# Block solutions of a gated DeltaNet layer: four systems in four column groups, two chunk pairs in one visit

## The chip, the cores and the metric

The kernel runs on one core of a Trainium2 chip. The metric is the device time of one execution in microseconds (us). The engines are the matrix engine (TensorE, PE in the profile; its weight loads are PEld), VectorE (DVE), ScalarE (ACT), GpSimd (POOL) and SyncE (SP), which issues the DMAs. Each engine works through its instructions in program order and waits on semaphores for the others.

## The reference, cut to what matters

One inference step of two layers, a sliding-window attention layer and a gated DeltaNet (GDN) layer, for 1024 prompt tokens and 8 x 4 sample tokens, model width 1024. The change is in the prompt part of the GDN layer:

```python
def gated_delta_chunked(q, k, v, g, beta, s0, chunk):
    ...
    decay = jnp.exp(jnp.where(incl, gc[..., :, None] - gc[..., None, :], -jnp.inf))
    kb = kc * bc[..., None]
    lower = jnp.where(strict, jnp.einsum('nbhik,nbhjk->nbhij', kb, kc) * decay, 0.0)
    rhs = jnp.concatenate([vc * bc[..., None], kb * jnp.exp(gc)[..., None]], axis=-1)
    sol = lax.linalg.triangular_solve(lower + jnp.eye(chunk, dtype=lower.dtype), rhs,
                                      left_side=True, lower=True, unit_diagonal=True)
    ...
    def step(S, xs):
        w_v_c, w_k_c, qk_c, q_dec_c, k_dec_c, g_tot_c = xs
        u = w_v_c - jnp.einsum('bhck,bhkv->bhcv', w_k_c, S)
        o = jnp.einsum('bhck,bhkv->bhcv', q_dec_c, S) + jnp.einsum('bhij,bhjv->bhiv', qk_c, u)
        S = S * g_tot_c[..., None, None] + jnp.einsum('bhck,bhcv->bhkv', k_dec_c, u)
        return S, o
```

Each value head and chunk has a unit lower triangular system. The kernel uses chunks of 128 tokens (the result does not depend on the chunk): 8 chunks, 16 value heads in 8 head pairs (two value heads share one key head), so 16 systems of 128 x 128 for each head pair. It inverts them once and then runs through the chunks in order, with the state `S`.

## The kernel before

The matrix engine's main work in this layer is the input projection. Column tiles of 128 columns are taken one after another in `plan`; each is 24 matmuls in float32r for each of three token groups (384, 384 and 288 columns; `ps_pj` in the profile, with weights `wh`, `wl` and activations `h2hi`, `h2lo`). For a head pair r the program projects q, two z tiles, the next pair's k, and two v tiles.

Everything else of the layer is written as generators that are woven in between those matmuls (`weave`). The program is laid out at build time: a planner (`Core`) keeps an estimated clock for each engine, and after each projection matmul it lets every generator go on whose next condition holds (`ready`, `soon`, `idle`). Where several could go on, ranks set by hand for each head pair (`KR`) decide. Conditions also hold the projection back (`until`): the k tile of pair r+1 is projected once the chain of pair r-1 is finished, and the pre-activation buffers of the convolution must be free. While it is held back, only woven work is laid out. What comes out is a fixed order for each engine.

For a head pair hq:

- `solve`: transposes of kT (`turn_sum`), key products `kT kT` in PSUM, and their scaled, decayed copy `UZ` (16 systems, four to a chunk pair: two chunks, two heads). The four 32 x 32 diagonal blocks of each system go to DRAM (`Ld`).
- `invert`: all 64 diagonal blocks are inverted at once on VectorE, in 31 steps of two instructions (`tmp`, `X`); the result goes through DRAM (`Xdd`) to `Xc`.
- `blocks`: for a chunk pair, the inverted blocks are masked into `Xd` (GpSimd), multiplied into `M` (PE, four matmuls; copied by ACT), and a 32 x 32 transpose writes them onto the diagonal of `UZ` (VectorE). Three steps of block substitution then fill the rows from 64, 32 and 0 on: each is a visit of four matmuls with 32-column weights `M` and 32, 64 or 96 moving columns of `UZ`, and a copy back. Two `blocks` generators run side by side, each with two chunk pairs one after the other. All four matmuls of a visit write the PSUM partitions of the rows that they fill.
- `decayed`: transposes and products of qT with kT, scaled into `DP`.
- `chain`: chunk by chunk `vo`, u (`ps_ob<-vo,UZ`), `us`, the state update (`us,ktok`), outputs (`S,qT`, `uo,DP`) and `S,kT` for the next chunk; each step alternates between PE and DVE or ACT.

The step in `blocks` that the change rewrites:

```python
                        rs, cs = slice(r0, r0 + 32), slice(r0 + 32, P)
                        for q in range(4):
                            nc.tensor.matmul(pzv[rs, q, cs], M[:, q, rs], uz[:, q, cs], start=True, stop=True)
                        yield soon(pz)
                        nc.vector.tensor_copy(uz[rs, :, cs], pzv[rs, :, cs])
```

After the last column tile the program waits for all `solve`, `invert`, `blocks` and `decayed` work, and then starts the output projection, with the rest of the last chain and the samples woven in. All instructions that pass the planner have line L89 in the profile, so one goes by tile names.

## Time and profile before

| | |
|---|---|
| median of 3 runs | 1768.01 us (1766.73 to 1768.91) |
| the profiled execution | 1762.72 us, span 1760.8 us |
| PE busy | 1670.2 us (95% of the span) |
| PEld busy | 1450.0 us (82%) |
| DVE busy | 1214.9 us (69%) |
| ACT busy | 864.3 us (49%) |
| POOL busy | 603.6 us (34%) |
| mean granted PE clock | 0.986 |

A row of the timeline is start, length, engine, line, operation, output and inputs, form and count; rows of one tile in a row are merged. Matmul ends are modelled, so lengths overlap; the time that a visit takes is read from start to start. A float32 matmul has two records.

### The profile page before, as it was taken

The page shows a single profiled execution, that of the slowest core. Times are in us where ns is not written, and L with a number is a line of the kernel's source. Part 1 is how long each engine was busy: PE and PEld are TensorE (multiplying, and loading weights), DVE is VectorE, ACT ScalarE, POOL GpSimd, SP SyncE. Part 2 cuts the span into 40 slices and gives each one's busy share as a digit, 9 for nine tenths or more (in the row PEclk, how much of TensorE's full clock was granted, in tenths as well). Part 3 has the DMA queues.
Part 4 walks back from the last instruction along what each step waited for, and adds up shares of the span by engine and source line. Part 5 has one row for each costly group of instructions (what it writes and reads, how often), then busy time and mean ns, then how long its engine had stood idle before and what let it go on. Part 6 is the DMA issues. An engine that isn't in the chain of part 4 may idle for free. (4 is left out here: it accounts for less than half of the span.)

```text
span 1760.8 us, 31819 instructions
## 1 busy us (share of the span) xinstructions
PE 1670.2 (95%) x10666; PEld 1450.0 (82%) x10666; DVE 1214.9 (69%) x3538; ACT 864.3 (49%) x2514; POOL 603.6 (34%) x1170
## 2 busy tenths in 40 slices
PE   6999999999998989799999999999999998998897
PEld 5988888877777889679999999899998987766685
DVE  5426676554555678867878778688697884458677
ACT  5525565453334555156554655564656564433332
POOL 2401110112122234344443544444344445323332
PEclk9999999999999999899999999999999999999999
DMA  9442121233333232132422324224133126764885
GB/s 338 131 112 61 49 69 49 67 103 110 102 108 101 62 88 61 52 87 53 115 61 70 95 62 112 60 67 120 39 94 82 45 76 187 240 193 145 265 258 168
DMA packets 281572, 191.77 MB, mean 109 GB/s; under 512 B 98361, under 2 KB 253881, under 8 KB 281378
## 3 DMA queue, kind: packets, MB, share of 16 engines
q1 hardware_dynamic: 281410, 189.75, 37.5%
q8 instruction: 84, 1.38, 0.3%
q14 instruction: 78, 0.64, 0.1%
HBM read 144.68 MB, written 47.04 MB: 109 GB/s over the span
## 5 line engine op out<-in xcount | busy, mean ns | idle before, releaser
L89 PE MATMUL ps_pj<-h2hi,wl 128*128 128x384 f32 (+1 forms) x1128 | 381.1, 338 | 2.7 <-POOL wl L89 2.5
L89 PE MATMUL ps_pj<-h2lo,wh 128*128 128x384 f32 (+1 forms) x1128 | 381.3, 338 | 0.0
L89 PE MATMUL ps_pj<-h2hi,wh 128*128 128x384 f32 (+1 forms) x1128 | 379.4, 336 | 0.6 <-ACT XR L89 0.6
L89 POOL TENSOR_TENSOR wl<-wr,wh 128x512 fp32r<-128x512 f32 x122 | 164.8, 1352 | 545.7 <-ACT wh L89 518.8
L89 PEld LDWEIGHTS ps_pj<-h2hi,wl 128*128 128x128 f32 x1128 | 213.7, 189 | 6.9 <-POOL wl L89 3.6
L89 PEld LDWEIGHTS ps_pj<-h2hi,wh 128*128 128x128 f32 x1128 | 213.5, 189 | 3.9 <-ACT XR L89 0.9
L89 PEld LDWEIGHTS ps_pj<-h2lo,wh 128*128 128x128 f32 x1128 | 213.6, 189 | 3.7
L89 POOL TENSOR_TENSOR xt<-xt,y 128x512 f32<-128x512 f32 (+1 forms) x48 | 63.3, 1323 | 176.0 <-DVE y L89 137.6
L89 PE MATMUL ps_pj<-hlo,wh 128*128 128x384 f32 (+1 forms) x360 | 119.6, 332 | 0.0
L89 PE MATMUL ps_pj<-hhi,wh 128*128 128x384 f32 (+1 forms) x360 | 118.6, 330 | 0.0
L89 PE MATMUL ps_pj<-hhi,wl 128*128 128x384 f32 (+1 forms) x360 | 118.0, 328 | 0.0
L89 DVE SCALAR_TENSOR_TENSOR vT<-XR,cT,vT 128x384 f32<-128x384 f32 (+1 forms) x144 | 90.3, 640 | 37.9 <-ACT vT L89 36.0
L89 DVE TENSOR_TENSOR tmp<-X 64x31 f32<-64x31 f32 (+15 forms) x248 | 91.2, 368 | 15.5 <-POOL X L89 12.3
L89 DVE TENSOR_TENSOR X<-X,tmp 64x31 f32<-64x31 f32 (+15 forms) x248 | 95.2, 384 | 8.5
L89 ACT CAST wh<-wr 128x512 fp32r<-128x512 f32 x122 | 75.1, 616 | 20.9 <-PE ps_pj L89 15.6
L89 PEld LDWEIGHTS ps_pj<-hlo,wh 128*128 128x128 f32 x360 | 67.8, 188 | 13.6 <-issue 13.5
L89 ACT COPY XR<-ps_pj 128x384 f32<-128x384 f32 (+1 forms) x96 | 43.2, 450 | 68.8 <-PE ps_pj L89 68.6
L89 PEld LDWEIGHTS ps_pj<-hhi,wh 128*128 128x128 f32 x360 | 67.7, 188 | 5.9 <-issue 4.2
L89 ACT ACTIVATE qe<-ps_mi,Eg 128x128 f32<-128x128 f32 x112 | 35.1, 364 | 74.4 <-PE ps_mi L89 74.4
L89 PEld LDWEIGHTS ps_pj<-hhi,wl 128*128 128x128 f32 x360 | 67.8, 188 | 3.3 <-issue 3.3
L89 ACT ACTIVATE prob<-prob,nm 128x256 f32<-128x256 f32 (+1 forms) x128 | 62.3, 489 | 11.3 <-DVE nm L89 11.1
L89 POOL TENSOR_TENSOR rst<-rsw 128x4 f32<-128x4 f32 x96 | 22.6, 235 | 128.7 <-DVE rsw L89 106.0
(580 smaller groups left out, 4330.4 us busy)
## 6 DMA issues: line engine op xcount, KB each, us to landing
wr<-in_gdn_w_in SPq DMA_DIRECT2D x96, 256.0 KB
S<-in_state_gdn_s SPq DMA_DIRECT2D x40, 256.0 KB
xt<-in_x_prompt SPq DMA_DIRECT2D x16, 512.0 KB
wm<-in_w_mod SPq DMA_DIRECT2D x16, 512.0 KB
wr<-in_swa_w_in SPq DMA_DIRECT2D x64, 128.0 KB
wm<-in_w_mod SPq DMA_DIRECT2D x32, 256.0 KB
wmod<-in_w_mod SPq DMA_DIRECT2D x32, 256.0 KB
DP<-gcr SPq DMA_DIRECT2D x64, 128.0 KB
```

Of the source, the lines that this page charges most:

```text
L89: inst = fn(*args, **kwargs)
```

## The change

The four `UZ` tiles of a head pair become one tile `full` of [128, 4, 4, 128] (chunk pair, system, columns). One `blocks` generator takes two chunk pairs at a time. A solution step is one visit of eight matmuls for both chunk pairs: system q of each writes PSUM partitions 32q to 32q+31, that is column group q of the array, and the two chunk pairs lie side by side in the columns. The copy back is four instructions, one for each q, from partitions 32q to the rows r0, for both chunk pairs: even q on VectorE, odd q on ScalarE. `decayed` waits for all products instead of for the fourth tile, and uses a scratch tile of its own in `turn_sum`. The ranks and the planner's costs stay.

```diff
-                jk = gs.tile([P, P], F32, tag="jk", name="jk")
+                jk = gs.tile([P, P], F32, tag="jk" if ktok is None else "jn", name="jk")
...
+            full = st["UZf"] = half(hq).tile([P, 4, 4, P], F32, tag="UZ", name="UZ", bufs=1)
+            nc.wide[full.tensor.name] = 8 * P
...
-                    ut = half(hq).tile([P, 2, 2, P], F32, tag="UZ", name="UZ", bufs=4)
+                    uv = full[:, cp_]
+                    ut = uv.rearrange("p (h c) i -> p h c i", h=2)
...
+            st["built"] = True
             weave(invert(hq, st, Ld, Xdd), "invert", hq)
...
-            def blocks(par):
-                for cp_ in (par, par + 2):
-                    xd = Xd[par]
+            def blocks():
+                for c2 in range(2):
                     yield soon(Xc)
-                    for b in range(4):
...
+                    for xd, cp_ in zip(Xd, (2 * c2, 2 * c2 + 1)):
+                        for b in range(4):
...
+                    Ms = []
+                    for xd, cp_ in zip(Xd, (2 * c2, 2 * c2 + 1)):
+                        yield ready(xd)
+                        pm = yield from bank(lg)
...
                     for r0 in (64, 32, 0):
-                        yield ready(M, uz)
+                        yield ready(*Ms, full[:, 2 * c2])
                         pz = yield from bank(lg)
-                        pzv = pz.rearrange("p (q i) -> p q i", q=4)
-                        rs, cs = slice(r0, r0 + 32), slice(r0 + 32, P)
+                        rs, cs, n = slice(r0, r0 + 32), slice(r0 + 32, P), 96 - r0
+                        pzv = pz[:, 0:2 * n].rearrange("p (s i) -> p s i", s=2)
+                        for s_, M in enumerate(Ms):
+                            for q in range(4):
+                                nc.tensor.matmul(pzv[32 * q:32 * q + 32, s_, :], M[:, q, rs], full[:, 2 * c2 + s_, q, cs],
+                                                 start=True, stop=True, skip_group_check=True)
+                        yield soon(pz)
                         for q in range(4):
-                            nc.tensor.matmul(pzv[rs, q, cs], M[:, q, rs], uz[:, q, cs], start=True, stop=True)
-                        yield soon(pz)
-                        nc.vector.tensor_copy(uz[rs, :, cs], pzv[rs, :, cs])
+                            d = full[rs, 2 * c2:2 * c2 + 2, q, cs]
+                            if q % 2:
+                                nc.scalar.copy(d, pzv[32 * q:32 * q + 32])
+                            else:
+                                nc.vector.tensor_copy(d, pzv[32 * q:32 * q + 32])
                         give(lg, pz)
-                st["ready"] = st.get("ready", 0) + 1
-                solved[0] += 1
...
+                st["ready"] = st.get("ready", 0) + 2
+                solved[0] += 2
...
-            yield lambda: st.get("qTdone") and "sj" in st and len(st["UZ"]) == 4
+            yield lambda: st.get("qTdone") and "built" in st
```

The planner lays all of the layer out anew. Three places of PE's order, and one of DVE's, follow; a count behind a row is of instructions.

Pair 4, first chunk pairs, PE, before (`Xd,UZ` is the product for `M`, `UZ,M` a solution step):

```order
L89 MATMUL ps_lg<-Xd_6510,UZ 128x96 x4
L89 MATMUL ps_pj<-h2hi,wh 128x384
L89 MATMUL ps_lg<-UZ,M 32x32 x4
L89 MATMUL ps_pj<-h2lo,wh 128x384
L89 MATMUL ps_pj<-h2hi,wl 128x384
L89 MATMUL ps_pj<-h2hi,wh 128x384
L89 MATMUL ps_pj<-h2lo,wh 128x384
L89 MATMUL ps_pj<-h2hi,wl 128x384
L89 MATMUL ps_lg<-UZ,M 32x32 x4
L89 MATMUL ps_pj<-h2hi,wh 128x384
L89 MATMUL ps_lg<-UZ,M 32x64 x4
```

Now:

```order
L89 MATMUL ps_lg<-UZ,M 32x32 x8
L89 MATMUL ps_pj<-h2hi,wl 128x384
L89 MATMUL ps_pj<-h2hi,wh 128x384
L89 MATMUL ps_pj<-h2lo,wh 128x384
L89 MATMUL ps_pj<-h2hi,wl 128x384
L89 MATMUL ps_pj<-h2hi,wh 128x384
L89 MATMUL ps_pj<-h2lo,wh 128x384
L89 MATMUL ps_pj<-h2hi,wl 128x384
L89 MATMUL ps_pj<-h2hi,wh 128x384
L89 MATMUL ps_pj<-h2lo,wh 128x384
L89 MATMUL ps_pj<-h2hi,wl 128x384
L89 MATMUL ps_lg<-UZ,M 32x64 x8
```

One visit of eight stands where two of four stood, with projections between the steps as before; pairs 2, 3, 5 and 6 have mostly the same picture.

Pair 0, PE, at the k projection of pair 2, which is held back until the chain of pair 0 is finished; before:

```order
L89 MATMUL ps_pj<-h2lo,wh 128x288
L89 MATMUL ps_pj<-h2hi,wl 128x288
L89 MATMUL ps_mi<-Xd_6510,UZ 128x96 x4
L89 MATMUL ps_mi<-UZ,M 32x32 x8
L89 MATMUL ps_mi<-UZ,M 32x64 x8
L89 MATMUL ps_mi<-UZ,M 32x96 x8
L89 MATMUL ps_ob<-vo,UZ 128x128 x2
L89 MATMUL ps_mi<-us,ktok 128x256
```

Now:

```order
L89 MATMUL ps_pj<-h2hi,wl 128x288
L89 MATMUL ps_lg<-qT,kT 128x128 x4
L89 MATMUL ps_mi<-Xd_6508,UZ 128x96 x4
L89 MATMUL ps_mi<-Xd_6510,UZ 128x96 x4
L89 MATMUL ps_mi<-UZ,M 32x32 x8
L89 MATMUL ps_mi<-UZ,M 32x64 x8
L89 MATMUL ps_mi<-UZ,M 32x96 x8
L89 MATMUL ps_mi<-Xd_6508,UZ 128x96 x4
L89 MATMUL ps_mi<-Xd_6510,UZ 128x96 x4
L89 MATMUL ps_mi<-UZ,M 32x32 x8
L89 MATMUL ps_mi<-UZ,M 32x64 x8
L89 MATMUL ps_mi<-UZ,M 32x96 x8
```

Before, 50 projection matmuls stand between the first product of pair 0 and this place; now all its blocks stand behind the last of them. At the end of the column tiles (pair 7) it is the same: all its blocks now stand behind the last projection.

Pair 5, chunk 3 of the chain, PE, before:

```order
L89 MATMUL ps_mi<-us,ktok 128x256
L89 MATMUL ps_pj<-h2lo,wh 128x384
L89 MATMUL ps_pj<-h2hi,wl 128x384
L89 MATMUL ps_tr<-cst,vo 128x128 x4
L89 MATMUL ps_mi<-S,qT 128x256
L89 MATMUL ps_mi<-uo,DP 128x128 x2
L89 MATMUL ps_pj<-h2hi,wh 128x384
L89 MATMUL ps_mi<-S,kT 128x256
L89 MATMUL ps_pj<-h2lo,wh 128x384
```

Now, from chunk 4 on, ahead of the k projection of pair 7:

```order
L89 MATMUL ps_pj<-h2hi,wl 128x288
L89 MATMUL ps_ob<-vo,UZ 128x128 x2
L89 MATMUL ps_mi<-us,ktok 128x256
L89 MATMUL ps_mi<-S,qT 128x256
L89 MATMUL ps_mi<-uo,DP 128x128 x2
L89 MATMUL ps_mi<-S,kT 128x256
L89 MATMUL ps_ob<-vo,UZ 128x128 x2
L89 MATMUL ps_tr<-cst,vo 128x128 x4
L89 MATMUL ps_mi<-us,ktok 128x256
```

and DVE in the same chunks:

```order
L89 TENSOR_SCALAR us<-ps_ob,sd 128x128 x2
L89 TENSOR_TENSOR tmp<-X 64x231
L89 TENSOR_TENSOR X<-X,tmp 64x11x21
L89 SCALAR_TENSOR_TENSOR mo<-mo,epq 128x4
L89 TENSOR_SCALAR rsw<-mo 128x4
L89 TENSOR_SCALAR rsw<-rsw 128x4
L89 SCALAR_TENSOR_TENSOR S<-S,Gt,ps_mi 128x128 x2
L89 TENSOR_TENSOR tmp<-X 64x220
L89 TENSOR_TENSOR X<-X,tmp 64x10x22
L89 TENSOR_TENSOR tmp<-X 64x207
L89 TENSOR_TENSOR X<-X,tmp 64x9x23
L89 SCALAR_TENSOR_TENSOR vo<-ps_mi,nEg,vo 128x128 x2
```

The last four chunks now stand with no projection between, and the inversion steps of pair 6 stand between their steps on DVE. Pair 2's last three chunks (ahead of the k projection of pair 4) stand alike, with transposes of qT, products of `decayed` and the products for `M` of pair 3 among them; and at one v projection each of pairs 3 and 4 three or four pieces of woven work stand in one row with no projection between.

36 lines of the change are left out of this document (16 added, 20 removed).

## The prediction

> **What bounds the kernel now.** I read the page first, then the busy time by stage, then the waits of the matrix engine (PE), then single visits in the timeline.
>
> ```profile
> span 1760.8 us, 31819 instructions
> PE 1670.2 (95%) x10666; PEld 1450.0 (82%) x10666; DVE 1214.9 (69%) x3538; ACT 864.3 (49%) x2514; POOL 603.6 (34%) x1170
> ```
>
> ```profile
> 707.00:781.00 74.00, 61.31 (x445) 48.56 (x444) 57.36 (x165) 23.13 (x79) 26.76 (x87) 0.93 0.26 69
> 781.00:1478.20 697.20, 683.63 (x4682) 640.11 (x4681) 550.39 (x1509) 399.05 (x1243) 321.49 (x779) 1.00 0.30 79
> ```
>
> The columns are the stretch, its length, the busy time of PE, its weight loads, DVE, ACT and POOL, the granted clock, and DMA. The edited code runs in these two stretches. From 781 to 1478 us, where head pairs 2 to 7 are solved, PE is busy 98% and VectorE (DVE) 79%. The waits of PE in that stretch:
>
> ```profile
> PE ps_tr L89 <- ACT vT L89: 3.5, 4, 1.7
> ...
> PE ps_pj L89 <- POOL wl L89: 0.2, 1, 0.2
> ```
>
> These are the first and last of seven (total, times, longest), 13 us together of 697. PE is the bound there: a PE microsecond saved is one of span, as long as projection matmuls (`ps_pj`) stand between the steps that wait for other engines. From 707 to 781 us it is otherwise:
>
> ```profile
> 722.04 1.03 PE L89 MATMUL ps_mi<-Xd,UZ 128*128 128x96 f32 x8
> ...
> 728.86 0.71 PE L89 MATMUL ps_ob<-vo,UZ 128*128 128x128 f32 x4
> ...
> 773.79 0.42 PE L89 MATMUL ps_pj<-h2hi,wh 128*128 128x384 f32 x1
> ```
>
> From 722.04 to 773.79 PE projects nothing; the chain of pair 0 runs from 728.86, and DVE, busy 57 of 74 us, sets the pace.
>
> The sum is made against the profiled execution (1762.7 us, span 1760.8), 5.3 us under the median 1768.0; I add the 5.3 at the end.
>
> **The solution visits.** A visit is four matmuls of one solution step, among projections:
>
> ```profile
> 709.01 0.34 PE L89 MATMUL ps_pj<-h2lo,wh 128*128 128x384 f32 x1
> 709.28 0.44 PE L89 MATMUL ps_mi<-UZ,M 128*32 128x32 f32 x8
> 709.64 0.44 PE L89 MATMUL ps_pj<-h2hi,wl 128*128 128x384 f32 x1
> ...
> 711.09 0.63 PE L89 MATMUL ps_mi<-UZ,M 128*32 128x64 f32 x8
> 711.65 0.44 PE L89 MATMUL ps_pj<-h2lo,wh 128*128 128x384 f32 x1
> 711.93 0.34 PE L89 MATMUL ps_pj<-h2hi,wl 128*128 128x384 f32 x1
> 712.10 0.34 PE L89 MATMUL ps_pj<-h2hi,wh 128*128 128x384 f32 x1
> ...
> 713.62 0.85 PE L89 MATMUL ps_mi<-UZ,M 128*32 128x96 f32 x8
> 714.40 0.44 PE L89 MATMUL ps_pj<-h2hi,wl 128*128 128x384 f32 x1
> ```
>
> From start to start a visit takes 0.36, 0.56 and 0.78 us for 32, 64 and 96 columns (two records for each matmul). A projection matmul takes 0.174 (711.93 to 712.10), but 0.27 ahead of a visit and 0.28 behind one, so each visit costs another 0.2. A head pair has four of each width: 4 x 1.70 = 6.8 us, and twelve crossings.
>
> Afterwards six visits hold eight matmuls each, going round the four column groups. Before has no such visit of these sizes; the nearest that go round four groups are these:
>
> ```profile
> 31.85 3.64 PE L350 MATMUL ps_mi<-wm,cT 128*32 128x512 f32 x32
> 394.24 0.33 PE L89 MATMUL ps_lg<-kxs,qz 64*32 64x32 f32 x16
> 394.39 0.62 PE L89 MATMUL ps_lg<-KT,qz 64*32 64x128 f32 x16
> 394.94 0.44 PE L89 MATMUL ps_pj<-hhi,wh 128*128 128x384 f32 x1
> ...
> 1497.37 0.64 PE L89 MATMUL ps_lg<-S,zq 128*32 128x256 f32 x8
> 1497.94 0.50 PE L89 MATMUL ps_pj<-h2hi,olo 128*128 128x512 f32 x1
> ```
>
> In one column group a record's time grows by 0.053 us per 64 columns ((0.78 - 0.36)/8 from 32 to 96), so 512 columns would take 0.43; the first row has 32 such records in 3.64, 0.11 each. Four groups do overlap. Sixteen records of 32 columns took 0.15 and of 128 columns 0.55, on half the rows of the array; eight of 256 columns, on all rows, 0.57. Scaled by columns both give about 0.15, 0.28 and 0.42 for the new visits. Bounds of a pair's six visits: 1.7 us by those rows, and 6.8 if a record costs 0.57/8 = 0.071 whatever its width (16 records are 1.14, six visits 6.8: no gain at all). I take 1.9, near the lower end, because the 32-column row shows records at 0.01. So 4.9 us are saved, and 1.0 for six crossings fewer (0.2 each, less because some visits of before stand together): 5.9 per pair.
>
> [...]
>
> **Evacuation.** Twelve DVE copies per pair become twelve smaller ones and twelve on ScalarE (ACT).
>
> ```profile
> L89 DVE COPY UZ<-ps_lg x84: 287/417/547, 763.4 to 1479.0; 32x128 f32<-32x128 f32 x28, 32x256 f32<-32x256 f32 x28, 32x384 f32<-32x384 f32 x28
> L89 POOL TENSOR_TENSOR Xd<-Xc,cst x128: 442/452/831, 703.7 to 1469.3; 32x128 f32<-32x128 f32 x128
> L89 DVE TENSOR_TENSOR tmp<-X x248: 172/356/1493, 637.6 to 1445.3; 64x31 f32<-64x31 f32 x8, 64x87 f32<-64x87 f32 x8, 64x135 f32<-64x135 f32 x8, 64x175 f32<-64x175 f32 x8
> L89 DVE TENSOR_TENSOR X<-X,tmp x248: 182/367/1523, 637.9 to 1445.5; 64x31 f32<-64x31 f32 x8, 64x87 f32<-64x87 f32 x8, 64x135 f32<-64x135 f32 x8, 64x175 f32<-64x175 f32 x8
> L89 ACT COPY XR<-ps_pj 128x384 f32<-128x384 f32 x64 | 30.5, 477 | 51.1 <-PE ps_pj L89 51.0
> ```
>
> DVE: before 4 x (0.29 + 0.42 + 0.55) = 5.0; after 4 x (0.22 + 0.29 + 0.35) = 3.4 at 64, 128 and 192 elements on the same slope: 1.6 less. ACT: twelve at 0.2 to 0.48 (the row is larger than any of them), about 3.5 us more per pair. Both lie beside PE work, since ACT is busy 399 of 697 us; without that cover a step waits for two copies in series, some 0.6 us. Eight GpSimd products now stand in one row instead of four: the weight splits behind them come up to 4 x 0.45 = 1.8 us later; they feed projections, and splits are made a column tile ahead. No DMA is added, and the joined tile takes the memory of the four. `decayed` starts at most four products (1.4 us) later; the chain also waits for the solutions, which end later. These cost nothing.
>
> **What moves.** The planner lays everything out anew with the old ranks. Five pairs (2 to 6) are solved among projections as before: 5 x 5.9 = 29.5 us gained. What is given back stands at places where the new order has no projection.
>
> Pair 5, last four chunks (ahead of the K projection of pair 7): chained steps alone, with the next pair's inversion in DVE's row. Chain steps alone before, by the start of `us`, and one chunk among projections:
>
> ```profile
> 736.46 0.59 DVE L89 TENSOR_SCALAR us<-ps_ob,sd 128x128 f32<-128x128 f32 x2
> 742.90 0.59 DVE L89 TENSOR_SCALAR us<-ps_ob,sd 128x128 f32<-128x128 f32 x2
> 752.59 0.61 DVE L89 TENSOR_SCALAR us<-ps_ob,sd 128x128 f32<-128x128 f32 x2 [0.25 <-PE ps_ob L89]
> 756.86 0.61 DVE L89 TENSOR_SCALAR us<-ps_ob,sd 128x128 f32<-128x128 f32 x2 [0.25 <-PE ps_ob L89]
> ```
>
> ```profile
> 971.33 0.61 PE L89 MATMUL ps_ob<-vo,UZ 128*128 128x128 f32 x4
> 971.70 0.42 PE L89 MATMUL ps_pj<-h2lo,wh 128*128 128x384 f32 x1
> ...
> 976.82 0.34 PE L89 MATMUL ps_pj<-h2hi,wl 128*128 128x384 f32 x1
> 976.99 0.60 PE L89 MATMUL ps_ob<-vo,UZ 128*128 128x128 f32 x4
> ```
>
> Alone a chunk takes 6.4 us with many inversion steps between, 4.8 on average over the next two (the inversion ends in the first), and 4.3 without. Among projections it is 5.66 us with 20 projections of 0.174 in it: 2.2. Three periods of 5.6 and an end of 2 are 19 us; the same work among projections would be 4 x 2.2 + 1.5 = 10. Given back: 9 (5 to 12). Pair 2, last three chunks, with more filled in (about 3.4 us of other PE work): 2 x 4.8 + 2.5 = 12 against 10: 2 (0 to 4). At two V projections (pairs 3 and 4) three transposes of `vT` and the next products stand with no projection between; by the longest such wait, 1.7 us, that is 2 and 4 (together 1 to 10).
>
> Pair 0: before, its blocks begin 50 projections ahead of the place without projections; now all of them stand in it. DVE there: 4 transposes (0.71 each, 2.8), some 18 inversion steps of 0.72 (13) and copies (3.4) in one row, 19 us; then the chain, 45 us as before (728.86 to 773.79), with pair 1's blocks inside; 65 projections of 0.174 and one more product, 12. That is 76 against the 74 us of the stretch quoted, although its visits are shorter; 3 with a slower clock (-5 to 8). Pair 7: all its blocks stand behind the last projection, two halves of 5.7 us (products 1.6, ACT and DVE round 1.3, three steps of 0.2 to 0.4 with 0.6 of copies) against 12 us now among projections: 0 (-4 to 4).
>
> The clock falls in such places. The longest wait of PE on `us` in the whole span, and two pieces of the place of pair 0:
>
> ```profile
> PE ps_mi L89 <- DVE us L89: 9.6, 11, 1.5
> ```
>
> ```profile
> 730.00:740.00 10.00, 5.93 (x21) 4.66 (x22) 9.52 (x29) 0.75 (x2) 0.00 (x0) 0.72 0.00 1
> 750.00:760.00 10.00, 7.44 (x37) 4.99 (x36) 5.88 (x21) 4.54 (x18) 4.41 (x17) 1.00 0.50 116
> ```
>
> The granted clock was 0.72 with PE busy 59% and 1.00 with 74%. At periods of 5 to 6 us I expect both; DVE hides most of it. [...]
>
> Everywhere else PE arrives 4% earlier while DVE has nearly the same work: (550 - 10)/668 = 81% instead of 79%. I add 4 us to the 13 of scattered waits (0 to 10).
>
> Sum: -29.5 + 9 + 2 + 6 + 3 + 0 + 4 = -5.5 us. 1762.7 - 5.5 + 5.3 = 1762.5; I predict 1763.
>
> **Rivals.**
> 1. The places without projections are cheap: if chunks there run at 4.3 us, pair 0's blocks finish with the inversion ahead of them, and scattered waits don't grow, 5 + 0 + 2 - 3 + 0 = 4 are given back: 25 gained, 1743. For it: 4.3 was seen. Against: the order puts inversion steps between.
> 2. DVE becomes the bound (slower): the last chunks at 6.4 (12), pair 2 4, V places 10, pair 0 8, scattered 10: 44 against 29.5, 1780 at most, 1775 likely. It decides from 5.9 us per pair given back on average. For it: DVE was 95% busy at 730 to 740 with PE at 59%, and the inversion is not made shorter. Against: 79% over the long stretch.
> 3. The gain is the crossings only (a record costs 0.071 whatever its width): 5 given by five pairs, 24 given back, 1787. Against: 0.01 per record at 394 us.
> 4. Loads of the four groups in line: a record cannot be faster than its load; in the quoted 3.64 us row 0.11 per record leaves that open, but in the 0.57 us one eight records took 0.071 each. At 0.071 it is rival 3's time, 1787. The 394 us rows load half the rows of the array and do not exclude it for 128; the 3.64 us row overlaps whole matmuls on 128. [...]
>
> **How the numbers follow.** A change of 0.2% (3.5 us) is about what a measurement of this kernel can tell. The forecast (net -13 to +3) has 0.45: 0.30 of it faster, 0.15 same. Rival 1 has 0.17, faster. Rival 2 has 0.28: 0.22 slower, 0.06 same. Rivals 3 and 4 together 0.10: 0.09 slower, 0.01 same. Faster 0.47, same 0.22, slower 0.31. The forecast's own range is 1755 to 1771. The range for 8 in 10 goes halfway and more into rivals 1 and 2: 1746 to 1781.
>
> **What would show it.** Right: the rows `UZ,M` drop to under 0.5 us from the start of a visit to the next projection at all three widths; the stretch with pairs 2 to 7 is shorter by 10 us or more although PE's waits in it go from 13 to about 30 us, most of them on DVE `us`, `S`, `vo` and ACT `vT`; the place without projections at pair 0 grows from 52 to about 62 us. Wrong: visits at 1.1 us (rivals 3, 4); PE waits as few as now (rival 1); PE waits over 45 us and DVE over 85% in the long stretch (rival 2). It would also be wrong if the last stage, from 1478 us, moves by more than a few us: I left it as it is.

## The result, and the profile after

The changed kernel takes 1809.96 us (median of 4 runs, 1807.78 to 1813.55) against 1767.37 for the kernel before on the same chip: a ratio of 1.0236 (95% interval 1.0217 to 1.0254), 42 us slower. 1763 was forecast, and the range ended at 1781.

The head of the page of the changed kernel, with busy time, share and instructions of each engine:

```profile
span 1809.0 us, 31894 instructions
PE 1667.1 (92%) x10666; PEld 1444.5 (80%) x10666; DVE 1200.5 (66%) x3538; ACT 888.9 (49%) x2610; POOL 594.0 (33%) x1170
```

The span grew by 48.2 us. PE's busy time fell by 3.1 and its idle time grew from 90.6 to 141.9, by 51.3. So the loss is waiting, not work. (The mean granted clock fell from 0.986 to 0.962, and matmuls at the lower clock count longer: sixteen records of the products `Xd,UZ` take 4.09 us at half clock in a row further down, against 1.03 for eight in the kernel before. That is one reason why so little of what the visits save shows in busy time.)

The stretches by stage: the place of pair 0 without projections, and from its end to the end of pair 7's blocks (length, busy PE, PEld, DVE, ACT, POOL, clock, DMA). Before:

```profile
721.90:773.80 51.90, 39.21 (x260) 29.95 (x258) 41.34 (x126) 17.66 (x63) 14.40 (x52) 0.90 0.22 58
773.80:1478.90 705.10, 691.53 (x4754) 646.30 (x4753) 556.24 (x1523) 402.24 (x1254) 323.55 (x784) 1.00 0.30 79
```

After:

```profile
705.40:788.90 83.50, 53.00 (x382) 40.49 (x381) 61.47 (x193) 24.06 (x85) 24.98 (x85) 0.69 0.19 43
788.90:1523.40 734.50, 684.53 (x4711) 638.28 (x4709) 545.89 (x1519) 424.40 (x1334) 326.01 (x798) 0.96 0.30 81
```

The place grew by 31.6 us and the long stretch by 29.4; the place begins 16.5 us earlier, because pair 0's blocks, which stood in part ahead of it, now stand in it. In the long stretch DVE went from 79% to 74%, so it didn't become the bound. What PE waits for from 705 to 1528 us after (total, times, longest):

```profile
PE ps_mi L89 <- POOL Xd L89: 13.6, 1, 13.6
PE ps_lg L89 <- POOL Xd L89: 13.0, 4, 7.4
PE ps_mi L89 <- DVE us L89: 10.7, 11, 1.6
PE ps_mi L89 <- DVE UZ L89: 7.4, 5, 2.4
PE ps_lg L89 <- ACT UZ L89: 5.4, 2, 2.8
```

All its rows together are 80.8 us; before, the same view from 707 to 1478.2 us sums to 25.3. The two rows at the top are new: PE waits for the masked inverse `Xd`, which comes late.

Among projections the visits did what was forecast (PE, pair 4's first chunk pairs, eight matmuls to a visit, two records each):

```profile
1132.86 0.33 PE L89 MATMUL ps_lg<-UZ,M 128*32 128x32 f32 x16
1133.12 0.44 PE L89 MATMUL ps_pj<-h2hi,wl 128*128 128x384 f32 x1
...
1135.06 0.43 PE L89 MATMUL ps_lg<-UZ,M 128*32 128x64 f32 x16
1135.42 0.45 PE L89 MATMUL ps_pj<-h2hi,wh 128*128 128x384 f32 x1
...
1138.23 0.54 PE L89 MATMUL ps_lg<-UZ,M 128*32 128x96 f32 x16
1138.69 0.57 PE L89 MATMUL ps_lg<-Xd,UZ 128*128 128x96 f32 x3
```

From start to start 0.26, 0.36 and 0.46 us for eight matmuls, against 0.36, 0.56 and 0.78 for four before: 2.2 us per pair instead of 6.8. Where the step before has only just ended, with no projections between, it is otherwise. A visit of pair 1's blocks, inside pair 0's place and at full clock:

```profile
784.15 1.50 PE L89 MATMUL ps_lg<-UZ,M 128*32 128x96 f32 x16
785.59 0.71 PE L89 MATMUL ps_ob<-vo,UZ 128*128 128x128 f32 x4
```

It takes 1.43 us. Its matmuls wait for the copies of the step before one by one: the first four start at 784.15, 784.53, 784.85 and 785.14, the last three of them just behind copies that end at 784.48, 784.79 and 785.09.

So most of the time went into places where PE has no projection. Their lengths, from the start of the last projection matmul ahead to that of the first behind (the forecast's 6 for the V projections was what they would be longer; they were 1.0 together before):

| place | forecast | before | after |
|---|---|---|---|
| pair 0 | 62 | 51.9 | 83.6 |
| pair 2, last chunks | 12 | under 3 | 16.0 |
| V projections, pairs 3 and 4 | 6 | under 1 each | 4.6 + 6.6 + 9.8 |
| pair 5, last chunks | 19 | under 3 | 23.2 |
| pair 7 | 12 | 12.8 (in two) | 33.6 |
| sum | 111 | | 177.4 |

### The profile page after: what moved, and what is told of

It is laid out like the page before. It is cut to its first block, busy times and chain, and to the rows that moved or that the text cites. A ratio compares the mean times of both kernels' runs of the same rounds, so it can differ in the third digit from the quotient of the medians.

```text
span 1809.0 us, 31894 instructions
## 1 busy us (share of the span) xinstructions
PE 1667.1 (92%) x10666; PEld 1444.5 (80%) x10666; DVE 1200.5 (66%) x3538; ACT 888.9 (49%) x2610; POOL 594.0 (33%) x1170
## 5 line engine op out<-in xcount | busy, mean ns | idle before, releaser
L89 PE MATMUL ps_pj<-h2lo,wh 128*128 128x384 f32 (+1 forms) x1128 | 377.0, 334 | 0.0
L89 DVE SCALAR_TENSOR_TENSOR vT<-XR,cT,vT 128x384 f32<-128x384 f32 (+1 forms) x144 | 96.4, 682 | 55.7 <-ACT vT L89 53.9
L89 PEld LDWEIGHTS ps_pj<-hlo,wh 128*128 128x128 f32 x360 | 67.7, 188 | 13.6 <-issue 13.5
L89 POOL TENSOR_TENSOR Xd<-Xc,cst 32x128 f32<-32x128 f32 x128 | 60.7, 474 | 29.5 <-DMA Xc<-Xdd 22.0
```

The source lines that it names most:

```text
L89: inst = fn(*args, **kwargs)
```

## Experiments

Ratios are to the kernel before, run on the same chip. Where an edit changes what the planner sees, it lays out another order, and that turned out to be most of the matter.

### Is it the instructions or the order?

**e1: the changed kernel with one number of the planner's bookkeeping changed.** `nc.wide` tells the planner how many columns of a joined tile it is to treat as one thing: 8 x 128 are two chunk pairs, 4 x 128 one. No instruction is added or removed but for the bookkeeping ones of another order.

```diff
-            nc.wide[full.tensor.name] = 8 * P
+            nc.wide[full.tensor.name] = 4 * P
```

> The changed kernel with one number changed: the planner's key of the joined tile covers one chunk pair (4 x 128 columns) instead of two (8 x 128). No instruction changes, only the planner's order. Theory A (the key): with the wide key the planner lets the products that fill a chunk pair wait for the transfers that read the pair beside it, so the inversion of pair 0 starts 140 projections later and the blocks of pairs 0 and 7 and the last chunks of pair 5 fall behind the last projection. By A the blocks go back to projections 605, 2908 and 3305, the waits of PE on Xd (26.6 us) vanish, and the cheap visits are left: before minus 25 to 33 us, 1735 to 1745. Theory B (the copies, or DVE, are the bound wherever the blocks stand): the visits hardly pay, 1765 to 1800. Theory C (the array: a record of the four groups costs as much as one group's): 1770 to 1790.

Measured: 1760.59 us, ratio 0.997 (0.9957 to 0.9983). One number of the layout gives back 49 us (47 by the ratios), and what is left of the change is 0.3% faster than before. That is far from theory A's 1735 to 1745.

```profile
span 1751.7 us, 31900 instructions
PE 1645.1 (94%) x10666; PEld 1430.1 (82%) x10666; DVE 1202.3 (69%) x3538; ACT 888.6 (51%) x2610; POOL 602.9 (34%) x1170
```

PE is busy 25.1 us less than before (the forecast said 29.5 for the visits), with the very instructions that in the order of the change came to 3.1 less. But its span is only 9.1 shorter: PE's idle time grew by 16.0, from 90.6 to 106.6. So even in this order most of what the visits save is waited for elsewhere.

**e5: the changed kernel without the column groups** (joined tile, wide key and the new wait of `decayed` kept; visits, copies and `blocks` as before). **e2: the kernel before with the joined tile alone** (there `decayed` keeps its old condition and may replace the decay factors before the last products have used them; so part of the result is computed with other factors).

```diff
 e5, against the changed kernel
-            def blocks():
-                for c2 in range(2):
+            def blocks(par):
+                for cp_ in (par, par + 2):
...
+                            nc.tensor.matmul(pzv[rs, q, cs], M[:, q, rs], uz[:, q, cs], start=True, stop=True)
+                        nc.vector.tensor_copy(uz[rs, :, cs], pzv[rs, :, cs])
 e2, against the kernel before
+            full = st["UZf"] = half(hq).tile([P, 4, 4, P], F32, tag="UZ", name="UZ", bufs=1)
+            nc.wide[full.tensor.name] = 8 * P
-                    ut = half(hq).tile([P, 2, 2, P], F32, tag="UZ", name="UZ", bufs=4)
+                    ut = full[:, cp_].rearrange("p (h c) i -> p h c i", h=2)
```

> The changed kernel without the column groups: the joined tile with its wide key and the later start of the decayed products, but two generators, one chunk pair in a visit, one column group and one DVE copy a visit, as before. It repeats the joined tile alone (1804.65 us), with the wait for the last product of the tile put back. If the key alone makes the loss, 1795 to 1808, and the difference to the changed kernel (1810) is what the visits brought less what they moved. If that first run was slow because the decayed products ran too early, it falls to 1770 to 1785.

> The kernel before with nothing but the joined tile and its wide key: visits in one column group, two generators, as before. Theory A (the key): pair 0's blocks lose their projections (604 to 648 of before become 648), the second half of pair 1's and 2's blocks move too, pair 7's stay at 3318 to 3361; so about the 8 us that the changed kernel had lost by the end of pair 1's chain, and 4 to 10 more for its longer visits without cover: 1776 to 1788. Theories B and C: the tile is innocent, 1765 to 1771.

Measured: e5 1805.49, 1.0213 (1.0184 to 1.0242), place of pair 0 86.7 us; e2 1804.65, 1.0218 (1.0198 to 1.0239), place 85.1. The joined tile with its wide key costs 38 us with no solution visit touched. e5 came as the key theory had it; e2 lies 17 us above what was expected of it.

**Where the key bites.** The sixteen scaled key products of pair 0 (`UZ<-ps_mi,sj,DP`) on DVE and the first inversion step (`tmp<-X`, 64x31) behind them; a row that has x8 is eight in one go. Before:

```profile
618.79 2.15 DVE L89 SCALAR_TENSOR_TENSOR UZ<-ps_mi,sj,DP 128x128 f32<-128x128 f32 x8
621.19 2.16 DVE L89 SCALAR_TENSOR_TENSOR UZ<-ps_mi,sj,DP 128x128 f32<-128x128 f32 x8 [0.24 <-PE ps_mi L89]
637.65 0.18 DVE L89 TENSOR_TENSOR tmp<-X 64x31 f32<-64x31 f32 x1 [3.60 <-POOL X L89]
```

The changed kernel:

```profile
616.29 2.15 DVE L89 SCALAR_TENSOR_TENSOR UZ<-ps_mi,sj,DP 128x128 f32<-128x128 f32 x8
622.85 1.39 DVE L89 SCALAR_TENSOR_TENSOR UZ<-ps_mi,sj,DP 128x128 f32<-128x128 f32 x5 [4.42 <-PE ps_mi L89]
628.24 0.34 DVE L89 SCALAR_TENSOR_TENSOR UZ<-ps_mi,sj,DP 128x128 f32<-128x128 f32 x1
645.12 0.35 DVE L89 SCALAR_TENSOR_TENSOR UZ<-ps_mi,sj,DP 128x128 f32<-128x128 f32 x1
646.70 0.34 DVE L89 SCALAR_TENSOR_TENSOR UZ<-ps_mi,sj,DP 128x128 f32<-128x128 f32 x1
657.30 0.18 DVE L89 TENSOR_TENSOR tmp<-X 64x31 f32<-64x31 f32 x1
```

e1:

```profile
616.67 4.45 DVE L89 SCALAR_TENSOR_TENSOR UZ<-ps_mi,sj,DP 128x128 f32<-128x128 f32 x16
633.32 0.18 DVE L89 TENSOR_TENSOR tmp<-X 64x31 f32<-64x31 f32 x1 [2.02 <-POOL X L89]
```

In `solve` a DMA reads the diagonal blocks of each finished chunk pair out of `UZ`. By the planner's code, with one key for two chunk pairs the plan takes the next product, which writes the other chunk pair, for a write into what the DMA still reads, and puts other work ahead of it. The last product ends 28 us after the first eight were done, and the inversion began 20 us later than before although projections ran earlier. Then the rest follows in PE's order:

```profile
705.75 0.72 PE L89 MATMUL ps_lg<-qT,kT 128*128 128x128 f32 x5
720.02 1.38 PE L89 MATMUL ps_mi<-Xd,UZ 128*128 128x96 f32 x5 [13.55 <-POOL Xd L89]
...
743.52 1.22 PE L89 MATMUL ps_ob<-vo,UZ 128*128 128x128 f32 x4
...
788.91 0.42 PE L89 MATMUL ps_pj<-h2hi,wh 128*128 128x384 f32 x1
```

and on GpSimd, where the product itself waits for the inverse on its way through DRAM:

```profile
718.25 0.44 POOL L89 TENSOR_TENSOR Xd<-Xc,cst 32x128 f32<-32x128 f32 x1 [12.18 <-DMA Xc<-Xdd]
```

Projections end at 705.3; 14.7 us pass until the first block product, the blocks take 23.5 (720.02 to 743.52), the chain 45.4.

**e18: narrow key for pair 0 alone.** From pair 2 on its order is that of the changed kernel.

```diff
-            nc.wide[full.tensor.name] = 8 * P
+            nc.wide[full.tensor.name] = (4 if hq == 0 else 8) * P
```

> The changed kernel with the narrow key (4 x 128) for head pair 0's joined tile alone; all other pairs keep the wide one (8 x 128). Its order differs from the changed kernel's only up to the 762nd projection matmul of the layer; from pair 2 on the steps stand at the same projections. Theory (the late products of pair 0 are what makes its place long): the sixteen products stand in one row on VectorE again, the inversion of pair 0 starts some 20 us earlier, the 13.6 us wait of PE on Xd falls below 5, the place goes from 83.6 to 62 to 74 us, and the time from 1810 to 1788 to 1800; the places of pairs 2 to 7 (16.0, 11.2, 9.9, 23.2, 33.6) stay within 3 us each, and they carry the other 27 to 37 us of the 49 that the narrow key gave on all pairs. Rival 1: all blocks of pair 0 still stand behind the last projection, so the place stays over 79 us and the time over 1804; pairs 2 to 7 carry nearly all. Rival 2: pair 0 carries nearly all, under 1775.

Measured: 1805.56 us, 1.0232 (1.021 to 1.0253): not told apart from the changed kernel. The inversion starts at 638.45 (18.9 us earlier), PE's wait ahead of the blocks is 1.8 us instead of 13.55, and the place falls to 69.2 us, as the theory had it:

```profile
638.45 0.18 DVE L89 TENSOR_TENSOR tmp<-X 64x31 f32<-64x31 f32 x1 [3.79 <-POOL X L89]
714.12 0.29 PE L89 MATMUL ps_pj<-h2hi,wl 128*128 128x288 f32 x1
716.22 1.83 PE L89 MATMUL ps_mi<-Xd,UZ 128*128 128x96 f32 x8 [1.80 <-POOL Xd L89]
783.35 0.42 PE L89 MATMUL ps_pj<-h2hi,wh 128*128 128x384 f32 x1
```

But the time did not follow: the place now begins at 714.1 instead of 705.3, so that 8.8 of the 14.4 us were only moved ahead of it, and 5.6 were won (place ends 783.3 and 788.9). The other places stayed (16.1, 4.7 + 6.5, 9.8, 23.6, 33.1). By the time of each projection against the kernel before, the changed kernel stands at +11.6 us behind pair 0's place and at +39.0 at the last projection compared; e1 goes from -6.5 to -15.7 over the same ones. Of their distance of 55, 18 arise up to the end of pair 0's place, of which this run won 6, and 37 behind it: 15 from there to the last projection, in pairs 1 to 6, and 22 at pair 7's place. The place went as the theory had it, the time as rival 1 had it.

The products are late in the other pairs too. Time from the start of a pair's first product to the end of its sixteenth, in us:

| pair | 0 | 1 | 2 | 3 | 4 | 5 | 6 | 7 |
|---|---|---|---|---|---|---|---|---|
| before | 4.6 | 9.0 | 7.5 | 5.5 | 4.2 | 7.1 | 9.9 | 7.4 |
| changed kernel | 30.8 | 15.0 | 20.3 | 11.3 | 8.0 | 20.2 | 18.8 | 9.4 |
| e1 | 4.5 | 9.2 | 8.5 | 4.9 | 4.7 | 9.2 | 14.3 | 7.3 |

That does not yet make them the cause of the time lost there. At pair 7 the key is not enough: e5 has the same key, and there the inversion of pair 7 begins behind 3109 projections (3130 before, 3219 in the changed kernel) and its place is 8.2 us long. In e5, 17 of the 38 us arise up to the end of pair 0's place and about 20 behind it, nearly all of them ahead of the last projection.

**e8 and e9: pair 0's inversion put first on DVE** (rank 21 to 0), in e1 and in the kernel before.

```diff
-    KR = [{'chain': 8, 'output': 9, 'solve': 5, 'invert': 21, 'blocks': 10, 'decayed': 0}, ...
+    KR = [{'chain': 8, 'output': 9, 'solve': 5, 'invert': 0, 'blocks': 10, 'decayed': 0}, ...
```

> The kernel with the narrow key and one rank changed: the inversion of pair 0 goes first (rank 0 instead of 21). The order then has the blocks of pair 0 at projections 384 to 463 and its chain at 506 to 648; no stretch of 58 us without projections is left, and pair 1's blocks stand at 864 to 937. In that stretch of the narrow key PE was busy 45 of 58 us, 9 us of that lost to the half clock: 13 + 9 = 22 us are to be had at most if PE is what bounds the rest. Theory A (what counts is whether projections stand between the steps): 12 to 22 us faster than the narrow key's 1760, 1738 to 1748. Theory B (DVE and the chain's length bound the kernel; what is saved at one place is waited for at the next): 0 to 6 us, 1754 to 1762.

> The kernel before with the same one rank (inversion of pair 0 first): blocks of pair 0 at projections 384 to 420, its chain at 468 to 630. In the 52 us without projections PE was busy 53 of 66 us (708 to 774), about 4 us of it lost to the half clock: 13 + 4 = 17 us at most. Theory A: 9 to 17 us faster than before, 1750 to 1758. Theory B: 0 to 5 us, 1762 to 1767. The difference to the narrow key with this rank is what the visits bring where no place is left without projections: 29 us by the prediction's sum, 5 to 10 if their gain is taken back by waits at the value projections.

Measured: e8 1777.89, 1.008 (1.0061 to 1.01); e9 1773.63, 1.0056 (1.0034 to 1.0078). Both are slower than the kernels they were made from, which no theory had. In e8 the blocks were put so early that PE ran into them among the projections:

```profile
PE ps_mi L89 <- POOL Xd L89: 19.3, 1, 19.3
```

So this earlier order was no gain: the plan had a step ready before the chip did.

### Does the clock make the place of pair 0 long?

Windows (length, busy PE, PEld, DVE, ACT, POOL, clock, DMA) of the changed kernel:

```profile
708.00:710.00 2.00, 0.00 (x0) 0.00 (x0) 1.81 (x6) 0.00 (x0) 0.00 (x0) 1.00 0.54 163
710.00:712.00 2.00, 0.00 (x0) 0.00 (x0) 1.79 (x7) 0.00 (x0) 0.00 (x0) 0.74 0.00 0
712.00:714.00 2.00, 0.00 (x0) 0.00 (x0) 1.83 (x9) 0.00 (x0) 0.00 (x0) 0.50 0.00 0
...
711.00:762.00 51.00, 28.89 (x168) 22.22 (x168) 37.80 (x121) 8.50 (x30) 12.05 (x42) 0.50 0.13 27
```

The clock halved in the idle of 13.55 us and stayed so for 51 us. **e6 and e7** put matmuls that nobody reads into pair 0's place to hold the clock up, in the changed kernel and in e1.

```diff
+    def warm(src, n, w=256):
+        t = psb("pj")
+        for _ in range(n):
+            nc.tensor.matmul(t[:, 0:w], src[:, 0:P], src[:, 0:w], start=True, stop=True)
 e6: ahead of the first products 13 of 512 columns, then two of 256 behind each visit and each u of pair 0
 e7: two of 256 behind the visits of the second half and behind each u of pair 0
```

> The changed kernel with work added to PE at pair 0's place alone: matmuls whose result nobody reads, 13 of 512 columns ahead of the first product of the blocks (into the wait of 13.6 us), 2 of 256 columns behind each solution visit and behind each product of UZ in the chain; the order of all other instructions is unchanged. In the changed kernel the clock was at half from 711 to 762 us, with PE busy 29 us of it. Theory D (the clock makes part of the loss): the clock stays full there, the blocks and the first three chunks run at the speed of the later ones, 14 us of busy time at most are saved, of which 4 or 5 are eaten where PE now arrives late: 8 to 11 us faster than the changed kernel, 1799 to 1802. Theory E (PE waits for DVE, ACT, GpSimd and transfers there, so that its speed doesn't matter): no gain, and the added matmuls delay it by 2 to 8 us, 1811 to 1818.

> The kernel with the narrow key and the same added matmuls at pair 0's place (2 of 256 columns behind each solution visit of its second half and behind each product of UZ in its chain; none ahead of the blocks, which have no long wait there). The narrow key had 24 us at half clock there, PE busy 18.6 us. Theory D: 4 to 8 us faster than the narrow key's 1760.6, 1752 to 1757. Theory E: 1760 to 1766.

Measured: e6 1807.49, 1.022 (1.0192 to 1.0249); e7 1759.98, 0.9965 (0.9946 to 0.9984). In e6 half-clock time at pair 0 falls from 51.2 to 13.6 us (mean granted clock of the execution 0.962 and 0.975) and the place goes from 83.6 to 83.0; in e7 from 24 to 6.8 (0.976 in e1, 0.979 in e7), and the place stays at 58.2. The lower clock in the place is real, but holding it up shortened nothing, as theory E had it: the place goes by its waits for `Xd`, DVE and GpSimd. (The filling matmuls stand in PE's row and may themselves cost part of what the clock gives; that was not separated.)

### What do the four copies cost?

**e4 and e17: all copies on DVE** instead of DVE and ACT in turn, in e1 (order laid out anew) and in the changed kernel (its order kept, by charging the planner the old costs).

```diff
-                            if q % 2:
-                                nc.scalar.copy(d, pzv[32 * q:32 * q + 32])
-                            else:
-                                nc.vector.tensor_copy(d, pzv[32 * q:32 * q + 32])
+                            nc.vector.tensor_copy(d, pzv[32 * q:32 * q + 32])
```

> As the kernel with the narrow key, but all four copies of a visit on DVE. In the profile of the changed kernel the copies of one visit go DVE, ACT, DVE, ACT, each waiting 0.25 to 0.4 us for the one before. Theory A: among projections this series is hidden, so DVE alone makes no difference beyond the new order: within 6 us of the narrow key with both engines. Theory B (copies and DVE bound): twelve more DVE copies of 0.28 us a pair are 3.4 us a pair, 20 to 27 us slower than with both engines.

> The changed kernel in its own order, with all four copies of a visit on DVE (the planner is still charged for two on ACT). In the changed kernel DVE waited 27 us (48 times) for ACT's copies and ACT 68 us (87 times) for DVE's. Theory H: 5 to 15 us faster than the changed kernel, 1795 to 1805; the order, with its stretches without projections, keeps the rest of the loss. If the turns of the copies cost nothing here: 1806 to 1814.

Measured: e4 1757.1, 0.9953 (0.9939 to 0.9968), the fastest of the kernels here that compute all of it, 0.5% faster than before; e17 1805.14, 1.0215 (1.0193 to 1.0237). Each lies a little under its parent, with intervals that overlap, so a gain from it is not shown.

**e3 and e12: column groups for one chunk pair at a time** (four matmuls and four copies in place of four matmuls and one), with the order laid out anew and with the order of before kept. **e16: e12 with all copies on DVE.**

```diff
 e3, e12, against the kernel before
-                            nc.tensor.matmul(pzv[rs, q, cs], M[:, q, rs], uz[:, q, cs], start=True, stop=True)
+                            nc.tensor.matmul(pz[32 * q:32 * q + 32, 0:n], M[:, q, rs], uz[:, q, cs], start=True, stop=True, skip_group_check=True)
...
-                        nc.vector.tensor_copy(uz[rs, :, cs], pzv[rs, :, cs])
+                        for q in range(4):
+                            if q % 2:
+                                nc.scalar.copy(uz[rs, q, cs], pz[32 * q:32 * q + 32, 0:n])
+                            else:
+                                nc.vector.tensor_copy(uz[rs, q, cs], pz[32 * q:32 * q + 32, 0:n])
 e16, against e12
-                            if q % 2:
...
+                            nc.vector.tensor_copy(uz[rs, q, cs], pz[32 * q:32 * q + 32, 0:n])
```

> The kernel before with nothing but the four column groups: four tiles, two generators, four matmuls in a visit, and four copies (even systems DVE, odd ones ACT) for each chunk pair. Theory A: the order keeps its places (blocks of pair 0 at 598, of pair 7 at 3332 to 3384), the matmuls of a pair's visits cost 1.9 instead of 6.8 us and the crossings stay, but there are 48 copies a pair instead of 12: before minus 15 to 25, 1743 to 1753. Theory B: the many copies in series (0.2 to 0.3 each) eat it, 1763 to 1785. Theory C: no gain from the array, 1768 to 1775.

> The column groups alone, as in the run that took 1797 us, but in the order of the kernel before: the planner is charged for each visit and its copies what the old visit and its one copy cost, so that every engine issues the same instructions in the same order as before, but for the visits' own matmuls and their copies (two on DVE, two on ACT instead of one on DVE). Theory F (the order drawn anew is what costs, the visits pay): visits of 0.20, 0.25 and 0.30 us instead of 0.36, 0.56 and 0.78 save 0.95 x 4 = 3.8 us a pair; five to seven pairs give 19 to 26 us, less some 2 to 4 for the longer series of copies: 1740 to 1750. Theory G (PE's time is not the bound; another engine or the chain's length is): 1760 to 1768.

> The column groups alone in the order of the kernel before, as in the run that took 1799 us, but with all four copies of a visit on DVE. In that run DVE waited 46 us (96 times) for ACT's copies and ACT 81 us (152 times) for DVE's, up to 3.8 us each, since the four go in turn. Theory H (the rows of the two engines are tied together by these copies, so that whatever stands ahead of a copy in ACT's row holds up DVE and PE): without it the visits' 19 us come out, less some 4 us for 0.4 us more DVE work a visit, 1745 to 1757. If it is the number of copies or the column groups themselves: 1780 to 1800.

Measured: e3 1796.92, 1.0179 (1.0157 to 1.0202); e12 1799.25, 1.0176 (1.0149 to 1.0202); e16 1777.51, 1.0058 (1.0039 to 1.0077). Neither of e12's theories came true. The order does not explain its time: it was kept. The waits of the copies for each other in e12, and of PE for them:

```profile
ACT UZ L89 <- DVE UZ L89: 80.6, 152, 2.6
DVE UZ L89 <- ACT UZ L89: 46.1, 96, 3.8
PE ps_lg L89 <- ACT UZ L89: 17.6, 21, 3.5
```

The four copies of a visit write one tile, and the program has them go in turn, each engine waiting for the other with its own row of work behind. Without the turns (e16) two thirds of e12's loss are gone (1.0176 to 1.0058); e16 lies between its two expectations. For the 10 us that stay the length of four copies in place of one is the likely reason:

```profile
L89 DVE COPY UZ<-ps_lg x336: 181/219/260, 770.2 to 1494.3; 32x32 f32<-32x32 f32 x56, 32x64 f32<-32x64 f32 x56, 32x96 f32<-32x96 f32 x56
...
PE ps_lg L89 <- DVE UZ L89: 14.2, 22, 1.9
```

Four at 0.22 are 0.88 us where one took 0.42 (median before), and PE's waits on DVE's `UZ` are 21.9 us (14.2, and 7.7 in `ps_mi`) against 3.4 before.

**e11: e1 with eight copies for a visit**, each chunk pair by itself, DVE and ACT one each.

```diff
-                        yield ready(*Ms, full[:, 2 * c2])
+                        yield ready(*Ms, full[:, 2 * c2], full[:, 2 * c2 + 1])
...
+                            nc.vector.tensor_copy(full[rs, 2 * c2, q, cs], pzv[32 * q:32 * q + 32, 0, :])
+                            nc.scalar.copy(full[rs, 2 * c2 + 1, q, cs], pzv[32 * q:32 * q + 32, 1, :])
```

> The narrow key with eight copies of half the size a visit: the four of the first chunk pair on DVE, the four of the second on ACT, so that the two engines work beside each other instead of in turn. In the narrow key a visit's four copies follow one another (about 1.0, 1.2 and 1.4 us for the three steps); here four of 0.17 to 0.22 in a row on each, 0.7 to 0.9. If the series of copies takes back the visits' gain: 4 to 10 us faster than the narrow key's 1760, 1750 to 1756. If it is hidden among projections: 1757 to 1765 (blocks of pairs 5 and 6 also move by some 50 projections).

Measured: 1797.8, 1.0185 (1.0162 to 1.0209), 37 us over e1, and both expectations were missed. DVE waits for ACT's copies 55.3 us (25.7 in e1) and ACT for DVE's 74.1 (62.7). At four copies for eight matmuls (e1) there is a small gain, at four for four (e12) or eight for eight (e11) a loss. That the turns cost is shown in a kept order (e12, e16), and so is that four copies on DVE take back more than the shorter visits give (e16). That the count alone decides is not: e11 also waits for both chunk pairs, and it and e1 have each an order of their own.

### Is PE the bound, and what is a new order worth by chance?

**e13 and e10: the kernel before with half the columns in each solution visit and its copy** (half of the off-diagonal solution is left out), with the order kept and with the order laid out anew.

```diff
+                        ch = slice(r0 + 32, r0 + 32 + (96 - r0) // 2)
-                            nc.tensor.matmul(pzv[rs, q, cs], M[:, q, rs], uz[:, q, cs], start=True, stop=True)
+                            nc.tensor.matmul(pzv[rs, q, ch], M[:, q, rs], uz[:, q, ch], start=True, stop=True)
-                        nc.vector.tensor_copy(uz[rs, :, cs], pzv[rs, :, cs])
+                        nc.vector.tensor_copy(uz[rs, :, ch], pzv[rs, :, ch])
```

> The kernel before with half the columns in its solution matmuls and copies (it leaves half of the off-diagonal solution out), again in the order of the kernel before. With the order drawn anew this work took 1772 us, 7 us more than before, with 18 us less on PE. Theory F: PE's saving of 2.5 us a pair comes out, 13 to 18 us, 1747 to 1753. Theory G: 1760 to 1767.

> The kernel before with half the columns in its solution matmuls and their copies (16, 32 and 48 instead of 32, 64 and 96): it leaves half of the off-diagonal solution out. Nothing else changes, so PE has 2.5 us less per pair (8 records x 0.053 us per 64 columns x 96/64 x 4) and DVE 1.8 us. Theory A: PE is the bound, so five to seven pairs give 13 to 18 us, 1748 to 1754. Theory B: the time that PE saves is waited for at other engines, 0 to 6 us, 1761 to 1767.

Measured: e13 1752.03, 0.9917 (0.9895 to 0.9939); e10 1771.95, 1.0041 (1.0029 to 1.0054). In e13 PE is busy 1658.0 us, 12.2 less than before, and the span is 1748.2, 12.6 shorter. That fits a microsecond of span for each of PE as long as the order stays. It does not part PE from DVE, since the copies are halved with the matmuls (DVE's 1.8 us a pair by the expectation of e10). The same instructions in an order laid out anew for their lower cost (e10) are 20 us slower.

**e14 and e15: the kernel before, with one cost in the planner changed** and nothing else (DVE's fixed cost 0.08 to 0.09; ACT's for a copy 0.06 to 0.07).

```diff
-                           "vector": (960, 0.13 if op == "scalar_tensor_tensor" else 0.08),
+                           "vector": (960, 0.13 if op == "scalar_tensor_tensor" else 0.09),
```

> The kernel before, every instruction the same, in another order: the planner's fixed cost of a DVE instruction is 0.09 instead of 0.08 us. Theory F (any order drawn anew is worse than the one that the ranks were set for): 5 to 35 us slower, 1770 to 1800. Theory G: within 4 us of before, 1761 to 1769.

> The kernel before, every instruction the same, in another order: the planner's fixed cost of a copy on ACT out of PSUM is 0.07 instead of 0.06 us. Theory F: 5 to 35 us slower, 1770 to 1800. Theory G: within 4 us of before, 1761 to 1769.

Measured: e14 1781.66, 1.0087 (1.006 to 1.0114); e15 1762.24, 0.9974 (0.9958 to 0.999). The same instructions in another order move the time by -5 to +15 us. e14 and e10 show that ranks set for one plan need not carry over to the next; e15 shows that they may.

## Why the prediction was wrong, point by point

**The step that failed** is "What moves", the price of the places without projections, and behind it the joined tile, which stood among the things that "cost nothing". The forecast's sum beside the two profiled executions, by how much later than before the same projection matmul starts:

| stretch | forecast | measured |
|---|---|---|
| up to the end of pair 0's place | 3 | 11.6 |
| from there to the last projection (visits, pairs 2 and 5, V projections, scattered waits) | -8.5 | 5.2 |
| pair 7's place and some 40 matmuls behind it | 0 | 22.2 |
| from there to the end | 0 | 9.2 |
| sum | -5.5 | 48.2 |

A move of the last stage is among the signs of being wrong that the prediction names; why the last stage grew stays open.

- **"A PE microsecond saved is one of span, as long as projection matmuls (`ps_pj`) stand between the steps that wait for other engines."** Borne out by e13 (12.2 of busy time, 12.6 of span, with DVE's copies halved too). Where the condition fails, or the copies go in turn, it does not hold: e1 has 25.1 less busy time and 9.1 less span.
- **The solution visits, 0.15, 0.28, 0.42 plus a crossing; 5.9 us per pair.** Right among projections: 0.26, 0.36 and 0.46 with the crossing in it; PE busy -25.1 in e1 (all eight pairs, at a mean clock of 0.976 against 0.986) where 29.5 was said for five. Rivals 3 and 4 fell: a visit of 1.1 us and more does occur, in the places, but there it waits for copies, and the sign that was named for them, such visits everywhere, did not come. Nor did the loads stand in line, as rival 4 had it: all sixteen loads of a visit use all rows, and at the median of 110 ns in the changed kernel's row of loads (below) sixteen in line would make 1.8 us; the visit took 0.26, with a load of 106 to 113 ns started about every 7 ns. The kernel before had this to show already: eight loads of 106 to 113 ns in a visit of 0.36 us, in one column group.

```profile
L89 PEld LDWEIGHTS ps_lg<-UZ,M x672: 106/110/178, 771.5 to 1523.0; 128*32 128x32 f32 x168
```

- **"These cost nothing": evacuation, joined tile, `decayed`.** This failed. The joined tile was costed as memory ("takes the memory of the four"), not as what the planner does with it. The line `nc.wide[...] = 8 * P` stands in the diff and was not priced; e1 and e5 show it to be 49 and 38 us, each in an order of its own. Of the evacuation "two copies in series, some 0.6 us" was named as the price without cover. The copies are in fact four in turn across two engines, each behind the other engine's row. In the changed kernel, with half as many copies as in e12, the turns are a small term (e17), so they were not what broke the forecast; e12 shows that they could have.
- **"What moves."** The right places were read from the order, and each was priced by its last chain alone. Pair 0's chain came to 45.4 us where 45 was said, and pair 5 to 23.2 where 19 was said. What was missing is the way up to a place: the inverse had not arrived. At pair 0, 14.7 us of 21.6 over the forecast pass ahead of the first product, on the inversion's last steps, its way through DRAM and the GpSimd products; and the blocks took 23.5 where DVE's row was summed to 19. The 0 for pair 7 failed in the same way; PE's rows there:

```profile
1493.97 0.29 PE L89 MATMUL ps_pj<-h2hi,wl 128*128 128x288 f32 x1
1501.69 4.09 PE L89 MATMUL ps_lg<-Xd,UZ 128*128 128x96 f32 x16 [7.43 <-POOL Xd L89]
...
1514.13 4.09 PE L89 MATMUL ps_lg<-Xd,UZ 128*128 128x96 f32 x16 [3.09 <-POOL Xd L89]
...
1527.54 0.47 PE L89 MATMUL ps_pj<-h2hi,ohi 128*128 128x512 f32 x1 [1.00 <-issue]
```

  7.4 us of waiting for `Xd` ahead of the first half and 3.1 ahead of the second; and the products that were costed at 1.6 us take 4.1 at half clock (the clock stood at half for 23.9 us of this place; no run tested what that costs here). A half takes 12.4 us, 3.1 of them the wait ahead of the second, instead of 5.7. The V projections became 20 us longer where 6 was said. Places together are 65 us over the forecast, the span 54 (1809.0 against 1760.8 - 5.5 = 1755.3); the rest came back among the projections and were not followed further.
- **Scattered waits, 4.** Outside the two `Xd` rows PE's waits grew by 29 us (54.2 against 25.3), some of them in the places; the split was not measured. Of the signs named for rival 2 one came (waits over 45 us) and one did not (DVE over 85%).
- **"The clock falls in such places ... DVE hides most of it."** Right for pair 0 so far as e6 and e7 show (mean clock 0.962 to 0.975 in e6 and 0.976 to 0.979 in e7, the place shorter by 0.6 us and not at all). There the clock dropped at 711 us, 4.5 us after the last matmul, in a gap of 13.55 us; in pair 5's last chunks it halved where no gap was longer than 1.35 us (below).
- **Rival 2, DVE as the bound.** The sign came as this rival had it, for another reason: DVE was 74% busy. Its sum was also off: 44 given back against 29.5 is 14.5 us slower, 1782.5 and not "1780 at most". Rival 1 (cheap places) fell.
- **Not thought of.** That the planner's redrawn order could be off as a whole. The forecast priced the few places where the new order has no projection, as if the remainder would run as before; e14 and e15 put -5 to +15 us on a new order of unchanged instructions, and that spread belonged in the range. It would not have held 42.

What is shown: the order laid out with the wide key costs 38 to 49 us (e1, e2, e5), well beyond the -5 to +15 of the two other orders tried; the products come late, and at pair 0 they make the inverse late and the place long (e18). In the changed kernel two thirds of the loss against e1 arise behind pair 0. What is only argued: that late products lead to it there as they do at pair 0. No run changed the key for one of those pairs alone, and pair 7's long place is not the key's alone: it is 33.6 us in the changed kernel, 8.2 in e5 with the same key, 8.6 in e1 and 21.6 in e4 with the narrow one.

## What to carry to other kernels

Where a planner lays out the order, a change of tile shape is a change of its dependency bookkeeping; compare the new order's first producers (here products, inversion, transfers) with the old ones ahead of pricing anything, and time the same instructions in the old order (e12, e13) to part the instruction's worth from the order's. Price an exposed place from the last producer far upstream to its last consumer, not from its own steps. And when a matmul layout splits one evacuation into several, count the copies and keep them on one engine where they would go in turn (e12 against e16: 1799.25 and 1777.51 us); here taking two chunk pairs at once halved their number, and of the kernels with column groups only such came out ahead of the kernel before (e1, e4, e7), by 0.5% at most.

## What the runs showed of the hardware that was not expected

- Four column groups with all 128 rows overlapped, weight loads too: eight float32 matmuls of 32 columns between two projections took 0.26 us, with sixteen loads of 106 to 113 ns in it, and of 96 columns 0.46, where four of 96 columns in one column group took 0.78.
- The granted clock dropped with no long idle. In pair 5's last chunks PE's longest gap was 1.35 us, and the clock was down in pieces from 1346 to 1356 us:

```profile
1344.00:1346.00 2.00, 0.72 (x4) 0.53 (x4) 1.90 (x7) 0.38 (x2) 1.18 (x5) 0.96 0.00 0
1346.00:1348.00 2.00, 1.93 (x6) 1.49 (x7) 1.49 (x5) 1.15 (x5) 0.00 (x0) 0.50 0.00 0
1348.00:1350.00 2.00, 2.00 (x9) 1.47 (x7) 1.79 (x7) 0.21 (x1) 0.00 (x0) 0.69 0.37 131
```

  Half-clock stretches of this trace are 3.41 us long or a multiple of that (6.8; 23.9 at pair 7's place; 51.2 at pair 0's), but for the last, which the end of the execution cuts off. PE was busy 36% in the 2 us in which it dropped; at pair 0, once it had dropped, PE at 57% did not lift it for 51 us. Cut into pieces of 3.41 us in step with these stretches, the trace shows PE busy 50% or less in each of the 15 pieces after which the clock fell, and 48% or more in every other piece at full clock; the clock rose again only behind pieces with 84% or more. The shares are rough, since matmul ends are modelled.
